# Gate, shift and scale of a conditioned trunk layer: matrix products on TensorE replaced by dot products on VectorE along a Hyena stage

## The chip, the cores and the metric

One core of a Trainium2 chip runs the whole program. The metric is the device time of one execution in microseconds (us), smaller is better. Before the change it is 3126.3 us, the median of three runs from 3124.62 to 3126.78.

The engines are named as in the profile: PE is TensorE (PEld its weight loads), DVE is VectorE, ACT is ScalarE, POOL is GpSimd, SP is SyncE, which issues most loads.

## The reference

One step of a backbone with two trunk layers, on 128 context tokens and 1024 latent tokens, model width D = 1024. Each layer first computes six vectors of width D from a condition, for the context (`c_ctx`) and for the latents (`c`):

```python
def adaln_mod(cond, w_ada, b_ada):
    m = jax.nn.silu(cond) @ w_ada + b_ada          # D -> 6 * D
    return jnp.split(m[:, None, :], 6, axis=-1)

hp = modulate(rmsnorm(xp, norm_w[i, 0]), mp[0], mp[1])
yp = mixer(hp)                                      # layer 0: hyena, layer 1: attention
xp = xp + mp[2] * rmsnorm(yp, norm_w[i, 1])
hp = modulate(rmsnorm(xp, norm_w[i, 2]), mp[3], mp[4])
xp = xp + mp[5] * rmsnorm(conv_ffn(hp, *ff), norm_w[i, 3])
```

and the same for the latents with `ms`. `modulate(h, s, c)` is `h * (1 + c) + s`. The change concerns vectors 2, 3 and 4 of layer 0: the gate of the first mixer, and the shift and the scale of the first feed-forward. The first mixer is Hyena: a product with a 1024 x 3072 matrix, a short convolution of three taps, a product of two of the three parts, a long convolution through a transform, and a product with the third part.

## The kernel before

All arithmetic is float32. A matrix product is made of three PE products, with each operand split into a rounded part `hi` and a remainder `lo`.

**The Hyena stage** is the loop `main` in `hyena()` (L1363), for j = 0 to 7 over blocks of 128 channels, with nine steps s each. In a step PE does one `group` (24 matmuls, L1340 to L1342: one third of the columns of one of the block's three parts, from the split weights `wr`). Then `short` of the group before is done: one ACT instruction (L1356) and two on DVE (L1357, L1358), from the bank in PSUM into `cb`. The rest of a step is spread over the block:

- s = 6: `Conv` multiplies two parts on DVE, `vxr` and `vxp` (through the helper at L951).
- s = 7: `turn` transposes them on PE (L1216, L1219), then `back` of the block before (L1268, L1273) goes back from the transform.
- s = 8: `base` transforms (L1232, L1237), a part of the filter network runs (L1132), and `unturn` transposes the result of the block before (L1283, L1286) into three PSUM banks.
- s = 0 of the next block: `gate` multiplies these banks with the third part on DVE (`yx`, `yxp`) and sends them off; `spread`, `mul` and `gather` are the butterflies and complex products on DVE at s = 0 to 5.

Instructions run on each engine in the order in which the code issues them. The order is written out by hand in this loop. Buffers come from pools with a planned place in memory, so an instruction may also wait for an earlier reader of the memory that it is to write.

**The vectors 2, 3 and 4** come from `Pipe` (L227) with `ada_items(0, (2, 3, 4), 2, ab1)`: 24 items, each half of the contraction of 256 of the 3072 columns. `pipe.step` starts one in steps s = 5, 6, 7 of blocks 0 to 6 and in s = 0, 1, 2 of block 7. An item loads 512 KB (`adar`, L310), two steps later splits it with two ACT instructions and an adding DMA issued by POOL (`halves`), one step later does 8 matmuls with `sc4`, the split and silu'd condition, as the stationary operand (L324), and every second item adds the bias on DVE (`m`, L331). For the gate the rows go to DRAM (L335), for shift and scale two PE transposes (L340) and two DVE instructions (L342, L343) put them into `ab`. So there are 12 additions at L331 and eight times two transposes.

Because each of these 8 matmuls goes with a `hi` or a `lo` of the condition in the four rows of `sc4`, the gate has four rows in DRAM, and `g_steps` loads and adds two halves for each of its two rows.

In a later stage the same kind of vectors is already computed in another way (`ada_rows`, L350 to L385): weights transposed, one row of 1024 per partition, and DVE multiplies a row by the broadcast condition and sums it in one instruction (L379).

Of the kernel before, what the change touches and what calls it, by code (L numbers as in the profile page):

```python
# [9 lines left out]
F32 = mybir.dt.float32  # L10
# [5 lines left out]
P = 128  # L16
# [141 lines left out]
def tile_step(tc, nc, a: dict, cst, mem, banks):  # L158
# [68 lines left out]
    class Pipe:  # L227


        def __init__(self, items):  # L230
            self.todo, self.live = iter(items), []

        def step(self, start=1):
            for g in list(self.live):
                if next(g, self) is self:
                    self.live.remove(g)
            for _ in range(start):
                g = next(self.todo, None)
                if g is not None:
                    next(g)  # L240
                    self.live.append(g)

        def drain(self, start=1):
            self.step(start)
            while self.live:
                self.step(start)


    sc4 = cst([P, KT, 4], F32R, "sc4")
    scf = cst([P, KT, 2], F32, "scf")  # L250

    def ada_setup():
        sync.dma_start(scf, a["cond"])
        act.activation(scf, scf, AF.Silu)
        split(sc4[:, :, 0:2], sc4[:, :, 2:4], scf)
# [50 lines left out]

    def ada_item(l, n, h, box, lead, ab):

        raw = bt([4, 256], "adar")
        sync.dma_start(raw, a["w_ada"][l, n, :, 4 * h:4 * h + 4, :])  # L310
        if h == 0:
            box["b4"] = st([256], "b4")[0:4]
            sync.dma_start(box["b4"], a["b_ada4"][l, :, n * 256:(n + 1) * 256])
        for _ in range(lead):
            yield
        ws = halves(raw, bt, [4, 256], True)
        del raw
        yield
        if h == 0:
            box["pt"] = ps("ada", True)  # L320
        pt = box["pt"]
        for k in range(4):
            for i, w in enumerate(ws):
                pe.matmul(pt[0:4, 0:256], sc4[:, 4 * h + k, :], w[:, k, :],  # L324
                          start=h == 0 and k == 0 and i == 0, stop=h == 1 and k == 3 and i == 1)
        del ws, w
        yield
        if h == 0:
            return
        m4 = st([256], "m4")[0:4]  # L330
        dve.tensor_tensor(out=m4, in0=pt[0:4, 0:256], in1=box.pop("b4"), op=ALU.add)  # L331
        unpin(box.pop("pt"))
        q, r = divmod(n, 4)
        if q % 3 == 2:
            pool.dma_start(m_d[l][q][:, 256 * r:256 * r + 256], m4)  # L335
            return
        yield
        pt = ps("adaT")
        for i in range(2):
            pe.transpose(pt[:, 4 * i:4 * i + 4], m4[:, P * i:P * i + P], ident[0:4, 0:4])  # L340
        m = st([2, 4], "mT")
        dve.tensor_copy(m, pt[:, 0:8].rearrange("p (i c) -> p i c", i=2))  # L342
        dve.tensor_tensor(out=ab[:, q % 3, :, 2 * r:2 * r + 2].rearrange("p c k -> p k c"),  # L343
                          in0=m[:, :, 0:2], in1=m[:, :, 2:4], op=ALU.add)

    def ada_items(l, qs, lead, ab):
        for q in qs:
            for r in range(4):
                box = {}
                for h in range(2):  # L350
                    yield ada_item(l, 4 * q + r, h, box, lead, ab)
# [55 lines left out]
    def g_steps(l, which, halves=False):  # L407

        wp = bt([D], "wp")
        sync.dma_start(wp, a["norm_w"][l, 2 * which + 1:2 * which + 2, :].partition_broadcast(P))  # L410
        gs, g2 = [bt([D], "G") for _ in range(2)], []
        src = m_d[l][3 * which + 2]
        for c in range(2):
            sync.dma_start(gs[c], src[c:c + 1, :].partition_broadcast(P))
            if halves:
                g2.append(bt([D], "g2"))
                sync.dma_start(g2[c], src[c + 2:c + 3, :].partition_broadcast(P))
        for g in gs:
            yield
            if halves:  # L420
                dve.tensor_tensor(out=g, in0=g, in1=g2.pop(0), op=ALU.add)
            dve.scalar_tensor_tensor(out=g, in0=g, scalar=32.0, in1=wp, op0=ALU.mult, op1=ALU.mult)
        yield gs
# [215 lines left out]


    SEVEN = ((0, 0), (4, 1), (5, 2), (3, 3), (1, 0), (6, 2), (2, 3))
    GROUPS = (3, 2, 2, 2, 2, 2, 2, 2, 2, 3)

    def ffn(l, hs, gs, nxt, queue, extra=iter(()), late=(), after=None):

        raw, spl, hid, accs = {}, {}, {}, {}
        ops, rows, sums, out = {}, {}, {}, {}
# [57 lines left out]
        def load_pair(j):  # L705
            if j < NJ:
                raw[j] = [bt([KT, P], "wr") for _ in range(2)]
                for i in range(2):
                    sync.dma_start(raw[j][i], a["ffn_up"][l, j, :, i])

        lo, hi = slice(0, 4), slice(4, 8)

        def total(i, j):

            a1, a2 = raw[j]
            x, y, op = ((a2[:, lo], a2[:, hi], ALU.add), (sums.get((1, j)), a1[:, lo], ALU.subtract),
                        (a1[:, lo], a2[:, lo], ALU.subtract), (a1[:, hi], sums.get((2, j)), ALU.subtract))[i - 1]
            t = sums[i, j] = bt([4, P], f"s{i}")
            dve.tensor_tensor(out=t, in0=x, in1=y, op=op)

        def weight(q, j):

            if q in (1, 2, 3, 6):
                return sums[{1: 2, 2: 3, 3: 1, 6: 4}[q], j]
            return raw[j][q == 5][:, lo if q == 0 else hi]

        def high(q, j):
            ops[j, q] = bt([4, P], "hi", F32R), bt([4, P], "lo", F32R)
            act.activation(ops[j, q][0], weight(q, j), AF.Copy)  # L729

        def low(q, j):
            dve.tensor_tensor(out=ops[j, q][1], in0=weight(q, j), in1=f(ops[j, q][0]), op=ALU.subtract)

        def both(q, j):
            ops[j, q] = halves(weight(q, j), bt, [4, P], True)

        def product(j, q):
            b, d = SEVEN[q]
            if q < 4:
                out[j, d] = ps("pp", True)  # L740
            pt = out[j, d]
            wh, wl = ops.pop((j, q))
            bh, bl = hs["pair"][b]
            for k in range(4):
                for i, (w, t) in enumerate(((wh, bh), (wh, bl), (wl, bh))):
                    pe.matmul(pt[:, 0:NP], w[:, k, :], t[:, k, :], start=q < 4 and k == 0 and i == 0,  # L746
                              stop=k == 3 and i == 2, skip_group_check=q > 3)

        def add(dst, x, pt):
            dve.tensor_tensor(out=dst, in0=pt, in1=x, op=ALU.add)  # L750

        def evac(q, j):
            if q == 0:
                u = sums["u", j] = st([NP], "u")
                act.activation(u, out[j, 0][:, 0:NP], AF.Copy)  # L755
                rows[j] = [st([2 * NP - 2], "row") for _ in range(2)]
            elif q == 1:
                pt, u = out.pop((j, 1)), sums["u", j]
# [1611 lines left out]
```

## Time and profile before

| what | us |
|---|---|
| device time, median of 3 runs | 3126.3 |
| the profiled execution | 3126.71 |
| its span, first to last instruction | 3124.9 |
| PE busy | 3044.9 (97%) |
| DVE busy | 2143.6 (69%) |
| ACT busy | 1729.7 (55%) |
| POOL busy | 619.2 (20%) |

The Hyena loop runs from about 50 to 562 us of this span, and its blocks begin (first matmul of step s = 0) at 50.79, 115.32, 176.43, 239.72, 301.21, 363.83, 431.30 and 494.07 us. These edges cut the stretches below. A row of a group of instructions gives the line, the engine, the operation, what it writes and reads, its size and, in square brackets, how long the engine sat idle before it and what ended that. A DVE instruction can start some ns before the one ahead of it has ended, so a slot is best read from start to start.

### The profile page before, as it was taken

To read this page: it belongs to the slowest core of one execution; us is meant where nothing else is said; L and a number is where in the kernel's file an instruction comes from. 1 tells how busy PE (TensorE), PEld (TensorE's weight loads), DVE (VectorE), ACT (ScalarE), POOL (GpSimd) and SP (SyncE) were. 2 spreads that over 40 slices of the span, in tenths; PEclk is the share of its full clock that TensorE was granted. 3 is DMA by queue.
4 is the path that set the end of the run, shared out by engine and by line. 5 is a ranking of instruction groups with operands and counts; after the bars stand their busy time and mean duration, and the time that the engine had idled before them with its cause. 6 is when DMAs were issued, how large, how long until landed. Compare 5 with 4: busy or idle time off the path is not lost. (4 is left out here: it accounts for less than half of the span.)

```text
span 3124.9 us, 46695 instructions
## 1 busy us (share of the span) xinstructions
PE 3044.9 (97%) x17332; PEld 2823.7 (90%) x17332; DVE 2143.6 (69%) x3057; ACT 1729.7 (55%) x3185; POOL 619.2 (20%) x1010
## 2 busy tenths in 40 slices
PE   8999999999998999999999999999999999999998
PEld 5999999778888999988899999999888998999987
DVE  5778888756676787776563347789565756777743
ACT  5454445545544777655533348899545546777532
POOL 3111111220001222211143422223220002222100
PEclk9999999999999999999999999999999999999999
DMA  6455546754445898777464464353363246887763
GB/s 254 114 125 119 125 114 157 212 187 141 149 156 154 211 214 209 168 290 258 149 196 148 134 194 110 96 145 106 135 212 140 96 161 153 215 183 182 218 212 119
DMA packets 190136, 520.48 MB, mean 167 GB/s; under 512 B 25730, under 2 KB 53986, under 8 KB 189908
## 3 DMA queue, kind: packets, MB, share of 16 engines
q1 hardware_dynamic: 137428, 394.94, 37.9%
q0 software_dynamic: 52480, 122.56, 19.5%
q8 instruction: 136, 2.23, 0.3%
q14 instruction: 92, 0.75, 0.1%
HBM read 354.50 MB, written 68.13 MB: 135 GB/s over the span
## 5 line engine op out<-in xcount | busy, mean ns | idle before, releaser
L746 PE MATMUL banks<-pair,hi 128*128 128x386 f32 x2464 | 639.1, 341 | 10.0 <-DVE junk L599 9.8
L746 PEld LDWEIGHTS banks<-pair,hi 128*128 128x128 f32 x2464 | 453.2, 190 | 11.4 <-DVE junk L599 10.7
L215 ACT ACTIVATE hi<-wr 128x1024 fp32r<-128x1024 f32 (+1 forms) x400 | 365.2, 913 | 150.4 <-DMA wr<-ffn_up 47.6
L220 DVE TENSOR_TENSOR lo<-wr,hi 128x1024 fp32r<-128x1024 f32 x247 | 305.4, 1237 | 204.8 <-ACT hi L215 203.4
L746 PE MATMUL banks<-pair,lo 128*128 128x386 f32 x1232 | 419.1, 340 | 0.7 <-DMA lo<-wr 0.7
L218 POOL DMA_DIRECT2D lo<-wr x153 | 132.5, 866 | 860.9 <-ACT lo L217 637.4
L690 PE MATMUL banks<-lo,hi 128*128 128x512 f32 x792 | 250.2, 396 | 5.9 <-DVE lo L220 5.9
L690 PE MATMUL banks<-hi,hi 128*128 128x512 f32 x792 | 251.7, 398 | 2.3 <-ACT hi L215 2.3
L690 PE MATMUL banks<-hi,lo 128*128 128x512 f32 x792 | 249.9, 395 | 0.0
L667 PE MATMUL banks<-hi,hi 128*128 128x388 f32 x704 | 240.6, 342 | 8.5 <-ACT hc L510 8.2
L669 PE MATMUL banks<-hi,lo 128*128 128x388 f32 x704 | 239.1, 340 | 1.8 <-DVE lo L220 1.8
L668 PE MATMUL banks<-lo,hi 128*128 128x388 f32 x704 | 239.7, 340 | 0.0
L746 PEld LDWEIGHTS banks<-pair,lo 128*128 128x128 f32 x1232 | 233.3, 189 | 1.0 <-DMA lo<-wr 1.0
L1746 DVE TENSOR_REDUCE mx<-banks 128x1 f32<-128x1152 f32 x128 | 173.4, 1356 | 68.9 <-PE banks L1741 61.7
L1340 PE MATMUL banks<-hi,hi 128*128 128x386 f32 (+1 forms) x576 | 200.4, 348 | 3.8 <-DVE hi L2072 2.5
L1342 PE MATMUL banks<-hi,lo 128*128 128x386 f32 (+1 forms) x576 | 197.1, 342 | 5.8 <-DMA lo<-wr 5.7
L1646 PE MATMUL banks<-hi,hi 128*128 128x384 f32 (+1 forms) x576 | 198.9, 345 | 0.0
L217 ACT ACTIVATE lo<-hi 128x512 fp32r<-128x512 f32 (+1 forms) x265 | 187.0, 706 | 18.6 <-DMA lo<-wr 6.2
L1648 PE MATMUL banks<-hi,lo 128*128 128x384 f32 (+1 forms) x576 | 196.0, 340 | 0.5 <-DVE lo L220 0.5
L1341 PE MATMUL banks<-lo,hi 128*128 128x386 f32 (+1 forms) x576 | 196.3, 341 | 0.0
L1647 PE MATMUL banks<-lo,hi 128*128 128x384 f32 (+1 forms) x576 | 195.9, 340 | 0.0
L690 PEld LDWEIGHTS banks<-lo,hi 128*128 128x128 f32 x792 | 148.8, 189 | 43.2 <-DVE lo L220 9.3
(386 smaller groups left out, 6869.5 us busy)
## 6 DMA issues: line engine op xcount, KB each, us to landing
wr<-ffn_up SPq DMA_DIRECT2D x176, 512.0 KB
wr<-ffn_down SPq DMA_DIRECT2D x132, 512.0 KB
lo<-wr POOLq DMA_DIRECT2D x132, 256.0 KB, 3.9
adaw<-w_adat SPq DMA_DIRECT2D x56, 512.0 KB
lo<-s POOLq DMA_DIRECT2D x88, 256.0 KB, 3.9
x<-x_d SPq DMA_DIRECT2D x33, 512.0 KB
hid<-cv SPq DMA_DIRECT2D x44, 384.0 KB
hd<-hid SPq DMA_DIRECT2D x88, 192.0 KB
```

The source lines that it names most:

```text
L215: act.activation(hi, src, AF.Copy)
L220: dve.tensor_tensor(out=lo, in0=src, in1=f(hi), op=ALU.subtract)
L667: pe.matmul(pt[:, 0:n], wh[:, k, :], hh[:, k, 0:n], start=k == 0, stop=False)
L668: pe.matmul(pt[:, 0:n], wh[:, k, :], hl[:, k, 0:n], start=False, stop=False)
L669: pe.matmul(pt[:, 0:n], wl[:, k, :], hh[:, k, 0:n], start=False, stop=k == KT - 1)
L690: pe.matmul(accs[c][i][h], s_[:, o:o + P], w_[:, 512 * h:512 * h + 512], start=first and n == 0, stop=last and n == len(parts) - 1)
L746: pe.matmul(pt[:, 0:NP], w[:, k, :], t[:, k, :], start=q < 4 and k == 0 and i == 0, stop=k == 3 and i == 2, skip_group_check=q > 3)
L1340: pe.matmul(pt[:, 0:n], wh[:, k, :], hh[:, k, 0:n], start=k == 0, stop=False)
L1341: pe.matmul(pt[:, 0:n], wh[:, k, :], hl[:, k, 0:n], start=False, stop=False)
L1342: pe.matmul(pt[:, 0:n], wl[:, k, :], hh[:, k, 0:n], start=False, stop=k == KT - 1)
L1646: pe.matmul(pt[:, 0:m], wh[:, k, :], hh[:, k, b:b + m], start=k == 0, stop=False)
L1648: pe.matmul(pt[:, 0:m], wl[:, k, :], hh[:, k, b:b + m], start=False, stop=k == KT - 1)
```

## The change

The three vectors are now computed by `ada_rows(0, (2, 3, 4), mcol[0])`: 24 steps, three vectors by eight blocks of 128 columns. Each loads 512 KB of the transposed weights (`adaw`, one step ahead), and DVE does two dot products, one for the context's and one for the latents' condition. The loop advances them in steps s = 0, 2, 4 and 6 of blocks 1 to 7: the first two advances load and silu the conditions (two ACT instructions), so the pairs of dot products stand in block 1 at s = 4 and 6, in blocks 2 to 6 at s = 0, 2, 4 and 6, and in block 7 at s = 0 and 2. After the loop the gate goes to DRAM by two PE transposes, one ACT instruction and one DMA (`gate_rows`), and `ab_from` builds the shift and the scale from `mcol`.

`Pipe`, its items, `sc4`, the bias `b_ada4` and the halves of the gate are gone. The code of the first product of the feed-forward is put into a class `Seven`; on DVE one sum and the preceding step's `finish` change places there, everything else stands in the same order. The core of the diff:

```diff
-    class Pipe:
-    def ada_item(l, n, h, box, lead, ab):
-        raw = bt([4, 256], "adar")
-        sync.dma_start(raw, a["w_ada"][l, n, :, 4 * h:4 * h + 4, :])
...
-        ws = halves(raw, bt, [4, 256], True)
...
-        for k in range(4):
-            for i, w in enumerate(ws):
-                pe.matmul(pt[0:4, 0:256], sc4[:, 4 * h + k, :], w[:, k, :],
...
-        dve.tensor_tensor(out=m4, in0=pt[0:4, 0:256], in1=box.pop("b4"), op=ALU.add)
...
-    def g_steps(l, which, halves=False):
+    def g_steps(l, which):
...
-        def main(filt, pipe, starts, between, tail):
+        def main(filt, rows, between, tail):
...
-                    pipe.step(starts(j, s))
+                    if j and s in (0, 2, 4, 6):
+                        next(rows, None)
...
-        pipe = Pipe(ada_items(0, (2, 3, 4), 2, ab1))
+        rows = ada_rows(0, (2, 3, 4), mcol[0])
...
-            pipe.drain(2)
-            wn = st([KT], "abw")
-            sync.dma_start(wn, a["nwc"][0, 1])
+            run(rows)
+            gate_rows(0, 2, mcol[0])
...
-            scale_ab(ab1, wn)
+            ab1 = ab_from(0, 1, mcol[0])
...
-            return op, make_g(0, 0, True), ab1
-        return main(filt, pipe, lambda j, s: 1 if s in ((0, 1, 2) if j == KT - 1 else (5, 6, 7)) else 0, between, tail)
+            return op, make_g(0, 0), ab1
+        return main(filt, rows, between, tail)
```

What a pair is, in the code that is now called here:

```python
junk = bt([D], "adaj")
for c in range(2):
    dve.scalar_tensor_tensor(out=junk if c == 0 else w, in0=w, scalar=1.0, in1=cb[c],
                             op0=ALU.mult, op1=ALU.mult, accum_out=mcol[:, q, k, c:c + 1])
```

DVE at the start of block 2, before (`m` is the bias addition, `yx` and `yxp` the gate of block 0, `hfb` the filter's taps, `fS` the first butterfly):

```order
168 L331 TENSOR_TENSOR m_1887<-banks,b_1100 4x256
169 L951 TENSOR_TENSOR yx_1907<-banks,cb_794 128x4x128 x2
170 L951 TENSOR_TENSOR yxp_1909<-banks,cb_794 128x128
171 L951 TENSOR_TENSOR hfb_1919<-banks,dec_1645 128x512 x2
172 L951 TENSOR_TENSOR fS_1936<-uA_1796,uB_1797 128x1024
```

and now, with the line numbers of the changed kernel (L1306 is `short`, L310 the dot products, L899 the helper):

```order
169 L1306 SCALAR_TENSOR_TENSOR cb_1556<-banks,hvec,cb_1556 128x384
170 L310 SCALAR_TENSOR_TENSOR adaj_1823,mcol_95<-adaw_1586,cb_1228 128x1024
171 L310 SCALAR_TENSOR_TENSOR adaw_1586,mcol_95<-adaw_1586,cb_1230 128x1024
172 L899 TENSOR_TENSOR yx_1827<-banks,cb_790 128x4x128 x2
173 L899 TENSOR_TENSOR yxp_1830<-banks,cb_790 128x128
174 L899 TENSOR_TENSOR hfb_1841<-banks,dec_1602 128x512 x2
```

The addition `m` is gone and a pair of dot products stands ahead of the gate and of everything behind it.

DVE at s = 6 of block 2, before (the last butterfly, `short`, and the product that `turn` transposes):

```order
212 L951 TENSOR_TENSOR fS_1936<-fS_1936,uA_1796 128x1024
213 L1357 SCALAR_TENSOR_TENSOR cb_2068<-banks,hvec,cb_2068 128x384
214 L1358 SCALAR_TENSOR_TENSOR cb_2068<-banks,hvec,cb_2068 128x384
215 L951 TENSOR_TENSOR vxr_2268<-cb_1857,cb_2068 128x128x8
216 L951 TENSOR_TENSOR vxp_2270<-cb_1857,cb_2068 128x128
```

and now:

```order
218 L899 TENSOR_TENSOR fS_1857<-fS_1857,uA_1728 128x1024
219 L1305 SCALAR_TENSOR_TENSOR cb_1981<-banks,hvec,cb_1981 128x384
220 L1306 SCALAR_TENSOR_TENSOR cb_1981<-banks,hvec,cb_1981 128x384
221 L310 SCALAR_TENSOR_TENSOR adaj_2189,mcol_95<-adaw_2068,cb_1228 128x1024
222 L310 SCALAR_TENSOR_TENSOR adaw_2068,mcol_95<-adaw_2068,cb_1230 128x1024
223 L899 TENSOR_TENSOR vxr_2193<-cb_1789,cb_1981 128x128x8
224 L899 TENSOR_TENSOR vxp_2195<-cb_1789,cb_1981 128x128
```

A pair stands directly ahead of `vxr`; nothing of the change stands between `vxp` and the next block's first `short`.

PE at s = 8 of block 2, before (the end of the last group, an item's matmuls, and `base`):

```order
981 L1342 MATMUL banks<-hi_764,lo_2149 128x386
982 L324 MATMUL banks<-hi_2319,sc_93 4x256
983 L324 MATMUL banks<-lo_2321,sc_93 4x256
984 L324 MATMUL banks<-hi_2319,sc_93 4x256
985 L324 MATMUL banks<-lo_2321,sc_93 4x256
986 L324 MATMUL banks<-hi_2319,sc_93 4x256
987 L324 MATMUL banks<-lo_2321,sc_93 4x256
988 L324 MATMUL banks<-hi_2319,sc_93 4x256
989 L324 MATMUL banks<-lo_2321,sc_93 4x256
990 L1232 MATMUL banks<-uT_2332,mat_457 128x128
```

and now:

```order
931 L1288 MATMUL banks<-hi_760,hi_2061 128x386
932 L1289 MATMUL banks<-lo_761,hi_2061 128x386
933 L1290 MATMUL banks<-hi_760,lo_2063 128x386
934 L1180 MATMUL banks<-uT_2243,mat_456 128x128
935 L1180 MATMUL banks<-uT_2243,mat_458 128x128
```

The item's eight matmuls are gone from PE; `base` follows the group at once.

## Rows read from the trace of the kernel before

**Rows 1.** Stretches: busy us (instructions) of PE, PEld, DVE, ACT, POOL; granted clock, DMA.

```profile
176.43:494.07 317.64, 311.83 (x2114) 303.88 (x2112) 267.02 (x469) 144.92 (x235) 48.67 (x63) 0.99 0.50 121
239.72:301.21 61.49, 61.40 (x423) 60.12 (x422) 52.72 (x92) 28.60 (x47) 10.24 (x13) 1.00 0.51 125
363.83:431.30 67.47, 64.49 (x426) 62.93 (x424) 53.37 (x94) 28.84 (x47) 10.17 (x12) 0.95 0.47 114
494.07:562.00 67.93, 65.37 (x444) 61.98 (x443) 57.23 (x103) 36.08 (x53) 12.77 (x16) 1.00 0.66 171
```

**Rows 2.** DVE's timeline in block 2: start, duration, operation [idle before].

```profile
177.28 0.40 DVE L331 TENSOR_TENSOR m<-banks,b 4x256 f32<-4x256 f32 x1
177.61 2.33 DVE L951 TENSOR_TENSOR yx<-banks,cb 128x512 f32<-128x512 f32 x2
...
181.76 1.23 DVE L951 TENSOR_TENSOR fS<-uA,uB 128x1024 f32<-128x1024 f32 x1 [0.44 <-PE banks L324]
...
185.94 0.62 DVE L1357 SCALAR_TENSOR_TENSOR cb<-banks,hvec,cb 128x385 f32<-128x385 f32 x1 [0.36 <-ACT cb L1356]
...
219.18 0.28 DVE L951 TENSOR_TENSOR vxp<-cb,cb 128x128 f32<-128x128 f32 x1
...
224.75 1.23 DVE L951 TENSOR_TENSOR fS<-kA,kA 128x1024 f32<-128x1024 f32 x1 [2.82 <-PE banks L1216]
...
239.38 0.62 DVE L1357 SCALAR_TENSOR_TENSOR cb<-banks,hvec,cb 128x384 f32<-128x384 f32 x1 [1.78 <-ACT cb L1356]
```

**Rows 3.** PE's timeline from `turn` of block 2 to block 3.

```profile
223.68 1.03 PE L1216 MATMUL banks<-ident,vxr 128*128 128x128 f32 x8
...
232.91 0.28 PE L324 MATMUL banks<-hi,sc 128*4 128x256 f32 x1
...
233.85 3.73 PE L1232 MATMUL banks<-uT,mat 128*128 128x128 f32 x32
...
239.72 0.42 PE L1340 MATMUL banks<-hi,hi 128*128 128x388 f32 x1
```

**Rows 4.** One stretch within block 2, columns as in rows 1.

```profile
188.66:219.46 30.80, 29.18 (x191) 28.55 (x190) 30.21 (x55) 8.46 (x15) 2.51 (x5) 1.00 0.52 144
```

**Rows 5.** DVE's timeline behind the loop, a pair of dot products and what follows.

```profile
620.69 1.22 DVE L379 SCALAR_TENSOR_TENSOR adaj<-adaw,cb 128x1024 f32<-128x1024 f32 x1
...
621.95 1.22 DVE L379 SCALAR_TENSOR_TENSOR adaw<-adaw,cb 128x1024 f32<-128x1024 f32 x1
...
623.10 0.32 DVE L447 CAST hi<-zero 128x8 fp32r<-128x8 f32 x3
```

**Rows 6.** Waits of PE, 100 to 640 us: total, times, longest.

```profile
PE banks L1342 <- DMA lo<-wr: 5.7, 5, 3.0
PE banks L1953 <- DMA w<-wo: 2.6, 1, 2.6
PE banks L324 <- DMA lo<-adar: 2.1, 2, 1.4
PE banks L1953 <- DMA w<-wor: 2.1, 1, 2.1
```

**Rows 7.** Two stretches in block 5, columns as in rows 1.

```profile
384.00:388.00 4.00, 2.67 (x8) 2.68 (x9) 3.93 (x6) 0.00 (x0) 0.00 (x0) 0.56 0.21 83
388.00:392.00 4.00, 4.00 (x15) 4.00 (x15) 3.90 (x6) 0.00 (x0) 0.00 (x0) 0.59 0.00 0
```

**Rows 8.** Block 7: waits of DVE up to 540.80, columns as in rows 6.

```profile
DVE cb L1357 <- ACT cb L1356: 3.7, 3, 1.8
DVE mT L342 <- PE banks L340: 1.0, 1, 1.0
DVE fS L951 <- PE banks L324: 0.8, 1, 0.8
```

**Rows 9.** DVE's timeline ahead of `turn` of block 7.

```profile
540.52 0.27 DVE L951 TENSOR_TENSOR vxp<-cb,cb 128x128 f32<-128x128 f32 x1
```

**Rows 10.** PE's timeline at `turn` of block 7.

```profile
543.96 1.04 PE L1216 MATMUL banks<-ident,vxr 128*128 128x128 f32 x8
```

More of the change, by code (lines that the diff above doesn't have):

```diff
@@ L225, in halves @@
         return hi, lo
-    class Pipe:
[L230 to L249, printed above, removed]
     scf = cst([P, KT, 2], F32, "scf")
@@ L405, in gate_rows @@
         pool.dma_start(m_d[l][q][0:2].rearrange("c (k p) -> k c p", p=P), r)
-    def g_steps(l, which, halves=False):
+    def g_steps(l, which):
         wp = bt([D], "wp")
         sync.dma_start(wp, a["norm_w"][l, 2 * which + 1:2 * which + 2, :].partition_broadcast(P))
-        gs, g2 = [bt([D], "G") for _ in range(2)], []
+        gs = [bt([D], "G") for _ in range(2)]
         src = m_d[l][3 * which + 2]
@@ L646, in ffn @@
         raw, spl, hid, accs = {}, {}, {}, {}
-        ops, rows, sums, out = {}, {}, {}, {}
+        rows = {}
         hid_d = [tc.dram_tile((P, 6 * P), F32, name=f"hid{l}_{j}") for j in range(NJ)]
@@ L702, in down0 @@
                     g == 0, g == NJ - 1)
[L705 to L747, printed above, removed]
@@ L779, in finish, with load_two, block @@
+        def load_two(j):
+            ws = [bt([KT, P], "wr") for _ in range(2)]
+            for i in range(2):
+                sync.dma_start(ws[i], a["ffn_up"][l, j, :, i])
+            return ws
+        def block(j, r, c):
+            if j not in rows:
+                rows[j] = [st([2 * NP - 2], "row") for _ in range(2)]
+            return rows[j][r][:, (NP - 1) * c:(NP - 1) * (c + 1)], slice(c, NP - 1 + c)
+        seven = Seven(NJ, NP, load_two, hs, block)
         def finish(j):
@@ L797, in side @@
                 rows[j][i] = rows.pop((j, i))
-        ALONG = (
-            ((-1, middle, 1), (0, total, 4), (-2, finish), (-1, evac, 6)),
-            ((-1, side, 1, 0), (-1, side, 1, 1), (1, both, 0), (0, high, 6), (0, evac, 0)),
-            ((3, load_pair), (-1, middle, 0), (2, total, 1), (0, low, 6), (0, evac, 1)),
-            ((1, both, 2), (-1, side, 0, 0), (2, total, 2), (0, evac, 2)),
-            ((2, high, 1), (1, both, 3), (-1, side, 0, 1), (0, evac, 3)),
-            ((2, low, 1), (1, both, 5), (0, evac, 4)),
-            ((-1, silu), (1, both, 4), (2, total, 3), (0, evac, 5)))
+        FILL = (((-1, middle, 1), (-2, finish)), ((-1, side, 1, 0), (-1, side, 1, 1)), ((-1, middle, 0),), ((-1, side, 0, 0),),
+                ((-1, side, 0, 1),), (), ((-1, silu),))
         def along(t):
             j, q = divmod(t, 7)
-            for d, fn, *args in ALONG[q]:
+            for d, fn, *args in FILL[q]:
                 if 0 <= j + d < NJ:
                     fn(*args, j + d)
+            seven.along(t)
         def along2(ts):
             for t in (next(ts), next(ts)):
-                if t >= -19:
+                if t >= Seven.FIRST:
                     along(t)
@@ L899, in main @@
                 j, q = divmod(t, 7)
-                product(j, q)
+                seven.product(j, q)
                 along(t)
@@ L1440, in main @@
             hs.clear()
[L1441 removed]
+            return tail(conv, mats)
         return hs, consts, load_mats, filter_mlp, Filter, load_w, split_w, main, yx_d
@@ L2005, in to_out @@
         return a["y_prompt"] if T == 0 else a["y_sample"][(T - 1) * P:T * P]
+    mcol = [mem([P, 6, KT, 2], F32, nm("mcol")) for l in range(2)]
     def prelude():
```

150 lines of the change are left out of this document (74 added, 76 removed).

## The prediction

> **What bounds the kernel now.** I read the stretches first, one for each block of the Hyena loop. In block 3 PE is busy for 61.40 of 61.49 us at the full clock, DVE for 52.72 and ACT for 28.60 [rows 1]: PE bounds the block, and 24 items of matmuls taken from it look like a plain gain. So the second view is the timeline of DVE within a block, to see where its other 8.8 us lie. From 188.66 to 219.46, the butterflies of block 2 up to `vxp`, DVE is busy for 30.21 of 30.80 us [rows 4]. Its idle time lies elsewhere: 2.82 us while it waits for `turn`, 1.78 ahead of the next block's first `short`, with smaller pieces between them [rows 2]. That is behind `vxp`, while PE does `turn`, `back`, the last group, `base` and `unturn`.
>
> So a block is a circle of two arcs. DVE's arc goes from the block's start, where it can take up the results of `unturn`, to the end of `vxp`: from 176.43 [rows 1] to 219.18 + 0.28 = 219.46 [rows 2], 43.0 us. Then PE's arc, from `turn` to the next block's start: 223.68 to 239.72 [rows 3], 16.0 us. In all 59.1, where the block takes 63.3. The difference, 223.68 - 219.46 = 4.2 us, is all that DVE may be late before it holds up `turn`, and all pairs of dot products stand on DVE's arc, none of them in its idle time. This decides the forecast.
>
> **The change part by part.** *Off PE.* Eight L324 matmuls take from 232.91 to 233.85, 0.94 us [rows 3]. Blocks 2 to 6 lose three items each, 2.82 us. A block without waits, block 3, then asks 61.49 - 2.82 = 58.7 us of PE; PE's arc loses one of the three and is 16.04 - 0.94 = 15.1. The waits for `lo<-adar`, 2.1 us in two [rows 6], go as well. If nothing took their place all of it would be won: 24 x 0.94 + 2.1 = 24.7 us, and a little for the 16 transposes.
>
> *Onto DVE.* A pair takes from 620.69 to 623.10, 2.41 us with its two readings of the sum [rows 5], the same form on the same 128x1024 operands. 24 of them are 57.8 us. Four in each of blocks 2 to 6: 9.64. What goes from DVE's arc: two additions `m`, 0.33 from start to start [rows 2], 0.66; and two waits, 0.44 for L324 and 0.36 for ACT [rows 2], since DVE is later there by a pair, 0.80. The arc becomes 43.0 - 0.66 - 0.80 + 9.64 = 51.2.
>
> These rows show 1.22 us for a dot product, just as long as other instructions of this size (`fS` 1.23 [rows 2]). The Trainium skill (Vector Engine (DVE) Microarchitecture Reference, section 7, Points that are easy to get wrong) says that this form with two sources in SBUF that aren't bf16 runs at half throughput. If that doubled the row's time, four pairs would take some 19 us and the block some 76; the row was taken with just such operands, so the trace already contains whatever there is of it, and I keep the row.
>
> *A block from 2 to 6.* 51.2 + 15.1 = 66.3 us, against PE's own 58.7. Before, these five took 317.64 us [rows 1]; 5 x 66.3 = 331.5, **+13.9 us**. PE now has 7.6 us in each block in which it waits. Some of that it will spend on `lo<-wr`, the remainder of the group's weights: 5.7 us in five waits before [rows 6], and PE comes 1.9 us earlier within the block, so I take 1.5 to 3.5 there. Some 0.5 to 1 goes at s = 1, where the banks of `unturn` come free a pair later because the gate is queued behind the pair. What is left, 2 to 5.5, is a wait for `vxr` at `turn`. Waits of PE ahead of DVE's arc cost nothing by themselves.
>
> *The granted clock.* They may cost something afterwards. Behind the 3.0 us wait for `lo<-wr` [rows 6] the clock stood at 0.56 and 0.59 for 8 us, with 8 and 15 matmuls [rows 7]: near the lower of its two levels, 1.2 GHz. Block 5, in which this lies, took 67.47; the other four took (317.64 - 67.47) / 4 = 62.5 [rows 1]. Of the 4.9 us between them the wait explains 2.3 to 3.0, and the slow clock about 2 to 2.6; I take 2.3. After a wait in the middle of a block this eats only slack now. After a wait at `turn` the slow matmuls lie on PE's arc, and the block grows to 68.6. With 2 to 5.5 us of wait at `turn` I count it for three of the five blocks, **+6.9 us**; bounds 0 and 5 x 2.6 = 13.
>
> *Blocks 0 and 1.* Block 0 loses one item and a wait of 2.1 - 1.4 = 0.7 [rows 6]: -1.6. In block 1 there are two pairs and no gate on DVE: 51.2 - 4.82 - 2.6 = 43.8 for its arc, the gate being `yx` and `yxp`, 2.33 + 0.28; PE needs 58.7 - 15.1 = 43.6 up to `turn`. The balance leaves about -0.5 there and -0.9 on PE's arc: together **-3.0**; bounds -4.5 and 0, since both engines arrive together.
>
> *Block 7.* `turn` came 543.96 - 494.07 = 49.9 us after the block's start [rows 1, 10], with five items of 0.94 and a 1.4 us wait [rows 6] ahead of it. DVE reached the end of `vxp` after 46.7 [rows 9]. It gains two pairs, 4.82, and loses three `m` and two pairs of L342/L343, about 1.5, and its waits inside the block, 3.7 - 1.8 (that one ends ahead of the block's start) + 1.0 + 0.8 = 3.7 [rows 8]: 46.3. PE without its items is earlier. **-3.5**; bounds -5 and -1.
>
> *What else moves.* Weight loads: 24 of 512 KB before and after, on SP's queue in other steps; 24 adding DMAs of POOL and 48 splits on ACT go, which had much room (28.60 of 61.49 [rows 1]). Behind the loop two additions of the gate's halves go, 1.2 each like other 128x1024 instructions, and two transposes and one ACT instruction come beside the out projection, which waits for weights there, 2.1 and 2.6 us [rows 6]. Those loads could come earlier, and buffers lie elsewhere in memory: **-1.0**; bounds -5 and +2. `finish` against one sum in the feed-forward: same work on DVE, beside a PE that is fed a step ahead: 0, bounds -1 and +1.
>
> **The sum.** 13.9 + 6.9 - 3.0 - 3.5 - 1.0 = +13.3 on the profiled execution's 3126.71, or 3140.0; that execution is 0.4 above the median, which changes nothing at this size.
>
> **The rivals.**
> *No slow clock at `turn`.* The same circle, but PE loses its slack in the middle of the block, in waits for `lo<-wr` and slow matmuls behind them, and comes to `turn` together with DVE. +6.4: 3133. For it: the longest such wait was already 3.0 with PE later [rows 6].
> *A slow clock at every `turn`*, and behind the one of block 1: 13.9 - 7.5 + 6 x 2.3 to 2.6 = +20 to +22, and up to +25 if waits for the new loads come on top: 3147 to 3152. For it: 7.6 us of slack must go somewhere, and one long wait of 3.0 brought the clock down [rows 6, 7]. The Trainium skill (TensorE: Matmul & The Clock Gate, section HAM oscillation — how this bites in real kernels) describes a loop which waits once in each turn and starts each burst at the throttled clock; by it this rival would be the likeliest. The trace of before has one such fall in these five blocks, so it shows the price, not that it repeats.
> *The dot products fit into DVE's idle time.* DVE's work in a block becomes 52.7 + 9.64 - 0.66 = 61.7 [rows 1], less than the 62.5 that a usual block takes. If pairs ran where DVE idles, blocks would last about 62 and PE's clock would hold: 5 x 62 - 317.64 = -7.6, with the other terms -15: 3112 to 3120, faster. It decides from the point where less than 4.2 us per block fall on DVE's arc, which would need two of the four pairs behind `vxp`. Against it: all four are issued ahead of `vxp`, the last directly ahead of `vxr`.
> *The pairs cost more than their row*, by waits for `adaw` or for an earlier reader of `adaj`'s memory: 0.5 us a pair is +10, 3150 and more.
>
> **How the numbers follow.** My forecast (some of the `turn`s with a slow clock, 3135 to 3146) 0.45; none 0.2; all 0.18; pairs that cost more, over 3152, 0.07; pairs in idle time, 3112 to 3120, 0.06; between that and the second case, by a gain behind the loop, 0.04. The likeliest gives 3140. From 3128 to 3152 the range leaves out the last three, about 0.17. A measurement tells 0.2%, 6.3 us, from no change: faster is under 3120.0, 0.06; within, up to 3132.6, takes three fifths of the case without slow clocks and the 0.04 below it, 0.16; slower 0.78.
>
> **What would show it.** Right: blocks 2 to 6 last 66 to 69 us each; DVE is busy for some 62 of them and nearly without a gap from the block's start to `vxp`; PE is busy less than 60 at full clock and waits for `vxr` at `turn`; the granted clock of these stretches falls under 1 where that wait is over 2 us; the Hyena stage is 10 to 16 us longer and the rest as it was. Wrong: `vxr` ready before PE comes to `turn`; a pair other than 2.4 us; blocks of under 63 us; or a stage behind the loop that moves by more than 5 us.

## The result and the profile after

The changed kernel takes 3145.0 us (median of four runs, 3142.1 to 3147.1) where the kernel before takes 3126.5 in the same comparison: 1.0059 times as long, 95% interval 1.0042 to 1.0077, so 18.5 us slower. The profiled execution, 3142.1 us with a span of 3139.8, is the fastest of its four; against the profiled execution of before it is 15.4 us longer.

The stretches of the Hyena loop, cut at the first matmul of each block. The first row is blocks 2 to 6 together and answers to the first of [rows 1]; then blocks 3, 4, 5. Columns as in [rows 1].

```profile
172.09:510.46 338.37, 308.38 (x1983) 303.58 (x1982) 308.02 (x533) 115.30 (x205) 28.41 (x45) 0.96 0.35 98
240.14:308.34 68.20, 60.86 (x400) 59.88 (x398) 61.71 (x108) 22.95 (x41) 5.68 (x9) 0.97 0.34 97
308.34:374.74 66.40, 60.91 (x400) 59.80 (x398) 61.58 (x107) 22.85 (x41) 5.67 (x9) 0.97 0.35 100
374.74:444.13 69.39, 63.79 (x399) 62.67 (x398) 61.69 (x108) 23.15 (x41) 5.69 (x9) 0.93 0.34 95
```

The five blocks last 338.4 us instead of 317.6. In block 3 PE was busy for 61.4 of 61.5 us before; now for 60.9 of 68.2, partly at a lower clock, and DVE for 61.7. The timeline of DVE in block 2, at its start and ahead of `vxp`, answers to [rows 2] and [rows 5]:

```profile
172.95 1.22 DVE L310 SCALAR_TENSOR_TENSOR adaj<-adaw,cb 128x1024 f32<-128x1024 f32 x1
...
174.21 1.23 DVE L310 SCALAR_TENSOR_TENSOR adaw<-adaw,cb 128x1024 f32<-128x1024 f32 x1
...
175.35 2.33 DVE L899 TENSOR_TENSOR yx<-banks,cb 128x512 f32<-128x512 f32 x2
...
218.94 1.22 DVE L310 SCALAR_TENSOR_TENSOR adaj<-adaw,cb 128x1024 f32<-128x1024 f32 x1
...
221.35 1.93 DVE L899 TENSOR_TENSOR vxr<-cb,cb 128x1024 f32<-128x1024 f32 x1
223.12 0.28 DVE L899 TENSOR_TENSOR vxp<-cb,cb 128x128 f32<-128x128 f32 x1
```

A pair takes 172.95 to 175.35 and 218.94 to 221.35, 2.40 and 2.41 us, with no wait ahead of it. From the block's start, 172.09, to the end of `vxp`, 223.40, DVE's arc is 51.3 us, where it was 43.0.

PE at `turn` of blocks 2 to 6 answers to the first of [rows 3]; before, it did not wait there:

```profile
223.34 1.06 PE L1164 MATMUL banks<-ident,vxr 128*128 128x128 f32 x6 [2.02 <-DVE vxr L899]
...
291.53 0.66 PE L1164 MATMUL banks<-ident,vxr 128*128 128x128 f32 x4 [4.37 <-DVE vxr L899]
...
359.57 0.66 PE L1164 MATMUL banks<-ident,vxr 128*128 128x128 f32 x4 [0.71 <-DVE vxr L899]
...
426.12 1.11 PE L1164 MATMUL banks<-ident,vxr 128*128 128x128 f32 x4 [3.04 <-DVE vxr L899]
...
495.29 0.87 PE L1164 MATMUL banks<-ident,vxr 128*128 128x128 f32 x6 [3.44 <-DVE vxr L899]
```

And the stretches from these five starts to the next block's start, PE's arc. The number ahead of the last two is the granted clock:

```profile
223.34:240.14 16.80, 16.80 (x122) 16.80 (x123) 11.47 (x23) 7.63 (x16) 0.39 (x1) 0.90 0.36 95
291.53:308.34 16.81, 16.81 (x123) 16.81 (x123) 11.50 (x23) 7.61 (x16) 0.39 (x1) 0.90 0.36 95
359.57:374.74 15.17, 15.17 (x123) 15.17 (x123) 11.50 (x23) 7.50 (x16) 0.34 (x1) 1.00 0.41 105
426.12:444.13 18.01, 18.01 (x122) 18.01 (x123) 11.50 (x23) 7.61 (x16) 0.38 (x1) 0.83 0.32 88
495.29:510.46 15.17, 15.17 (x122) 15.17 (x123) 11.49 (x23) 7.50 (x16) 0.39 (x1) 1.00 0.41 106
```

At full clock the arc is 15.17 us; in three of five blocks the clock fell behind the wait, and the arc is 1.6, 1.6 and 2.8 us longer. The clock in these rows is a mean over the arc: in block 5 the granted clock is 0.50, the 1.2 GHz level, from 426.12 to 432.00 and full from 434.00 on. PE's waits in these five blocks, which answer to [rows 6]:

```profile
PE banks L1290 <- DMA lo<-wr: 16.4, 7, 3.8
PE banks L1164 <- DVE vxr L899: 13.6, 5, 4.4
```

So PE has a second large wait beside the one for `vxr`: the weights' remainder `lo<-wr`, 16.4 us. Which of the two sets the block, the runs had to tell.

Behind the loop, the first matmul of the out projection comes at 572.63, before at 559.68 (L1902 and L1953 of the two kernels, from the timelines of PE):

```profile
572.63 1.20 PE L1902 MATMUL banks<-w,wo 128*128 128x512 f32 x4 [0.47 <-ACT wo L215]
```

```profile
559.68 1.20 PE L1953 MATMUL banks<-w,wo 128*128 128x512 f32 x4 [0.65 <-ACT wo L215]
```

That is +12.95 there; the span is +14.9 at its end.

### The profile page after: what moved, and what is told of

The parts are those of the page before. It is cut to its first block, busy times and chain, and to the rows that moved or that the text cites. A ratio compares the mean times of both kernels' runs of the same rounds, so it can differ in the third digit from the quotient of the medians.

```text
span 3139.8 us, 46118 instructions
## 1 busy us (share of the span) xinstructions
PE 3032.8 (97%) x17126; PEld 2815.8 (90%) x17126; DVE 2190.4 (70%) x3126; ACT 1684.2 (54%) x3139; POOL 587.0 (19%) x983
## 4 chain that ended last, share of the span: by engine, by line
PE 63%; DVE 3%; issue 2%; ACT 2%; DMA 2%; POOL 1%; SPq 0%; POOLq 0%; DVEq 0%; ACTq 0%
PE banks L629 20%; PE banks L704 15%; PE banks L1690 4%; PE banks L1721 4%; PE banks L1597 3%; PE banks L1596 3%; PE banks L1595 3%; PE banks L681 3%; PE banks L683 2%; PE banks L682 2%; PE banks L1711 2%; PE banks L1902 2%; DMA wr<-ffn_up 1%; DVE lo L220 1%; ACT hi L215 1%
## 5 line engine op out<-in xcount | busy, mean ns | idle before, releaser
L747 DVE SCALAR_TENSOR_TENSOR cv<-row,dw,cv 128x768 f32<-128x768 f32 x176 | 178.0, 1013 | 10.4 <-ACT cv L742 8.4
```

## The experiments

Each run is given with its ratio to the kernel before, measured beside it. The median of that kernel lay between 3124.6 and 3127.1 us in the five comparisons, so a difference between runs of two comparisons is uncertain by some 2.5 us.

Three theories stood against each other. **The circle:** a block is DVE's arc up to `vxp` and PE's arc behind `turn`; the pairs lengthen the first, slow clocks the second. **A:** PE's waits for `lo<-wr` set the block. **B:** the other loads or the other places of buffers in memory do.

### The pairs behind `vxp`

```diff
-                    if j and s in (0, 2, 4, 6):
-                        next(rows, None)
+                    if s in ((7, 8) if 1 < j < 7 else (0, 2, 4, 6) if j else ()):
+                        for _ in range(2 if 1 < j < 7 else 1):
+                            next(rows, None)
```

> The changed kernel with the place of the dot products alone moved: the four pairs of each of blocks 2 to 6 stand behind `vxp`, two at s = 7 and two at s = 8, where before the change DVE idled; blocks 1 and 7 as in the changed kernel. Same instructions, same loads. Theory (a block is DVE's arc up to `vxp` plus PE's arc from `turn` on, and the pairs lengthen the first): the pairs leave DVE's arc, DVE has 53.7 + 9.6 = 63.3 us of work in a block and no idle time left, blocks 2 to 6 take 62.5 to 64.5 instead of 67.7 on average, the five together about 318 instead of 338, the total 3122 to 3128, and PE no longer waits for `vxr`. Rival A (PE's waits for the weights' remainder `lo<-wr`, 18 us in all, set the block): these stay and so does the time, 3140 to 3147. Rival B (24 more loads or other places in memory): as A.

3132.3 us (3130.5 to 3133.8), 1.0022 times the kernel before (1.0013 to 1.0032): 12.7 us faster than the changed kernel, with the same instructions, but over the 3122 to 3128 expected. Blocks 2 to 6 together and block 5:

```profile
173.84:494.31 320.47, 300.76 (x1983) 297.99 (x1981) 305.69 (x527) 114.64 (x205) 28.64 (x45) 0.98 0.38 105
364.23:429.26 65.03, 60.49 (x400) 59.94 (x398) 61.66 (x108) 22.93 (x41) 5.72 (x9) 0.97 0.36 102
```

PE no longer waits for `vxr` in them. Place alone took 18 us out of the five blocks, which neither A nor B allows. But PE is busy for 60.5 of 65.0 us and DVE for 61.7, so neither fills the block: five waits for `lo<-wr`, 17.7 us, longest 4.2, and a slow clock behind them remain. So A is wrong as the cause in the changed kernel, and right as the next bound: beside these waits PE has only 2.0 us of others in the five blocks.

### No pairs at all

```diff
+            if l == 0 and qs == (2, 3, 4):
+                if n == 0:
+                    pool.memset(mcol, 0.0)
...
+                yield
+                continue
             for c in range(2):
                 dve.scalar_tensor_tensor(out=junk if c == 0 else w, in0=w, scalar=1.0, in1=cb[c],
```

The 24 pairs are passed over and their loads stay; the kernel leaves out this part of the vectors, which are zero plus the bias.

> The changed kernel without the 24 pairs of dot products; their loads stay, and the vectors are zero plus the bias, so this part of the computation is left out. Theory: DVE's arc shrinks to some 42 us, PE bounds the block again at 58.7 us and a wait of 1 to 3 for `lo<-wr`: blocks 2 to 6 take 59.5 to 62 us, together about 303 instead of 338, and block 7 some 2 less: 3104 to 3112, some 15 to 22 under the kernel before, which is what the change would bring if DVE had room. Rival A: the waits for `lo<-wr` stay at 2 to 3.8 us with slow clocks behind them, blocks 64 and more, over 3125. Rival B (the loads or places in memory): 3140 or more.

3115.6 us (3113.4 to 3119.4), 0.9973 (0.9960 to 0.9985): 8 to 9 us under the kernel before instead of the expected 15 to 22. The five blocks take 311.3 us, and in them PE waits only for one thing:

```profile
PE banks L1299 <- DMA lo<-wr: 12.3, 5, 3.2
```

The chain behind this wait can be read in the changed kernel at the start of block 3, in the timelines of DVE, ACT, POOL and PE, one line each:

```profile
248.25 1.36 DVE L899 TENSOR_TENSOR uA<-uA,uB 128x1024 f32<-128x1024 f32 x1
```

```profile
249.65 0.63 ACT L923 ACTIVATE uA<-uA 128x512 f32<-128x512 f32 x1 [9.85 <-DVE uA L899]
...
251.04 1.05 ACT L215 ACTIVATE hi<-wr 128x1024 fp32r<-128x1024 f32 x1
```

```profile
253.48 0.90 POOL L218 DMA_DIRECT2D lo<-wr  x1 [4.96 <-ACT lo L217]
```

```profile
259.64 0.44 PE L1290 MATMUL banks<-hi,lo 128*128 128x388 f32 x1 [2.97 <-DMA lo<-wr]
```

ACT scales the butterfly's half `uA` at s = 0, and waits for DVE for that; the split of the next group's weights is queued behind it, then POOL's adding DMA, and PE needs its result at s = 3. From the issue to PE's start it is 6.2 us. Before the change the same chain took 6.9 us from the issue, at 188.25, and ended 0.64 us late in block 2:

```profile
195.19 0.45 PE L1342 MATMUL banks<-hi,lo 128*128 128x388 f32 x1 [0.64 <-DMA lo<-wr]
```

Two of a block's three items of matmuls, 1.9 us, stood on PE ahead of this place; without them PE comes earlier, and these waits are 12.3 us in five blocks instead of 5.7. So the removed matmuls had been cover for a transfer, and of the 24.7 us that the prediction held possible for the matmuls and their own waits 8 to 9 were left. The next runs take this wait away.

### The split one step earlier

```diff
-                    elif c == 1:
+                    elif c == 0:
                         split_w(i + 1)
-                    elif c == 2:
+                    elif c == 1:
                         load_w(i + 2)
```

Now ACT splits ahead of the scaling. The edit was made to the changed kernel, to the one without pairs and to the kernel before.

> The changed kernel with the weights of the next group loaded and split one step earlier each, so that ACT splits ahead of the scaling that waits for DVE's butterfly at s = 0 and `lo<-wr` lands long before PE needs it. The pairs stay where the change put them. Theory (DVE's arc to `vxp`, 51.3 us, and PE's arc from `turn`, 15.1 and 16.8 to 18.0 behind a slow clock): PE no longer waits for `lo<-wr` but as much longer for `vxr`, 5 to 7 us; blocks 2 to 6 take 66.4 to 69 us as before, together 332 to 345; 3138 to 3152. Rival (in the changed kernel the waits for `lo<-wr` set the block, 14 to 18 us in all with the slow clock behind them): 3122 to 3132.

3151.4 us (3149.7 to 3151.9), 1.0081 (1.0066 to 1.0096). PE's waits in the five blocks, block 3, and PE's arc of block 2:

```profile
PE banks L1164 <- DVE vxp L899: 38.4, 5, 7.8
```

```profile
242.55:310.95 68.40, 60.55 (x400) 60.14 (x398) 61.68 (x108) 22.75 (x42) 5.73 (x9) 0.95 0.33 97
225.51:242.55 17.04, 17.04 (x122) 17.04 (x123) 11.41 (x22) 7.97 (x17) 0.00 (x0) 0.88 0.14 53
```

All of `lo<-wr` is gone, and the kernel is no faster: by the medians it is 6 us slower. This is the run that decides between the circle and A: every bit of slack now lies ahead of `turn`, 7.6 to 7.9 us in each block, the clock falls behind each of these waits, PE's arc is 16.9 to 17.0 in every block, and the five blocks take 341.4 us, each 51.3 + 17.0.

> The kernel without the pairs of dot products (their loads stay, the vectors are left without them), with the same earlier split. Theory: without the pairs the waits for `lo<-wr` had taken PE's place as the bound; without these too PE is the bound and works at full clock: blocks 2 to 6 at 58.7 to 59.5 us, together 294 to 298 where the kernel without the pairs took 311; 3097 to 3104, which is the whole 22 to 25 us of the removed matmuls. Rival (something else of the change, loads or places in memory, holds the blocks): 3110 to 3116.

3092.6 us (3090.3 to 3093.6), 0.9892 (0.9878 to 0.9907), below the expectation. Blocks 2 to 6 and block 3:

```profile
172.90:464.94 292.04, 292.04 (x1984) 291.88 (x1982) 261.23 (x453) 115.33 (x206) 30.14 (x45) 1.00 0.40 113
231.31:289.71 58.40, 58.40 (x400) 58.37 (x398) 52.32 (x92) 23.07 (x42) 6.01 (x9) 1.00 0.41 113
```

PE is busy for every moment of 292.0 us at full clock: 58.4 a block, where the prediction had worked out 58.7. The loads are those of the change, so they do not hold the loop. The buffers of the pairs live shorter here, so the places need not be the same; what speaks against these is the run before, in which the two arcs alone make up each block with all pairs in it.

> The kernel before the change with the earlier split alone. Theory: its five waits for `lo<-wr`, 5.7 us, and the one slow clock in block 5, 2 to 2.6, go; PE bounds every block of 2 to 6 at 61.4: together 307 to 309 instead of 317.6; 3115 to 3120. Rival (DVE's arc of 43 us plus PE's 16 already limits, or ACT is held up by the earlier split): 3122 to 3128.

3119.3 us (3114.4 to 3121.3), 0.9981 (0.9972 to 0.9990); the five blocks 309.6 instead of 317.6. So the earlier split gives 5 us without the change. The other 26.7 us (3119.3 to 3092.6) come from the change when its pairs are left out and nothing else holds the blocks: 24.7 had been worked out for the matmuls and their waits.

### Matmuls in PE's wait

```diff
                     pt = ps("ut")
+                    if g == 0 and 1 < self.j < 7:
+                        for i in range(24):        # the second run: range(9)
+                            pe.matmul(pt[:, 0:P], mats[0][:, i % 8, :], mats[1][:, i % 8, :], start=True, stop=True)
```

> The changed kernel with 24 more matmuls (128x128, their results unused, about 2.8 us) on PE directly ahead of `turn` in blocks 2 to 6, so that PE works while it would wait for `vxr`. Theory (behind the waits at `turn` the slow clock lengthens PE's arc in three of five blocks by 2 to 3 us): the waits fall under 2 us, no slow clock behind them, each block 66 to 66.8, the five together 331 to 334 instead of 338: 3135 to 3141, faster although PE does more. Rival (the clock behind the wait costs nothing, or another wait takes its place): 3143 to 3150, since in a block where PE came late the matmuls add up to 2.8 us.

3161.0 us (3158.9 to 3162.3). The 24 matmuls took 5.5 us instead of 2.8, since the trace shows two for each that is written, and held `turn` up themselves: it began 3.2 to 4.7 us after the end of `vxp`. The expectation fell through the size of the edit. The clock at `turn` it does show: PE has no wait there, and its arc is 15.1 us in all five blocks (228.16 to 243.27 in block 2).

> The changed kernel with 9 unused matmuls of 128x128 ahead of `turn` in blocks 2 to 6. In the run with 24 they took 5.5 us, twice as long as meant, and held `turn` up themselves; 9 take about 2.1. Theory (slow clock on PE's arc behind the wait at `turn`, 1.6 to 2.8 us in three of five blocks): waits at `turn` fall under 2 us, `turn` to the next block 15.2 in every block, five blocks together 331 to 337 instead of 338; 3137 to 3144. Rival: where PE comes late the matmuls hold `turn` up by up to 2 us, or the fall of the clock only moves to the waits for `lo<-wr`: 3144 to 3150.

3147.7 us (3145.9 to 3150.0), 1.0071 (1.0054 to 1.0087): not told apart from the changed kernel. PE's arc in four of the five blocks:

```profile
224.03:239.17 15.14, 15.13 (x121) 15.14 (x122) 11.45 (x23) 7.52 (x16) 0.35 (x1) 1.00 0.39 105
292.01:307.15 15.14, 15.14 (x125) 15.14 (x123) 10.20 (x20) 7.50 (x16) 0.00 (x0) 1.00 0.34 97
359.79:374.93 15.14, 15.14 (x124) 15.14 (x123) 10.16 (x20) 7.50 (x16) 0.00 (x0) 1.00 0.34 96
426.35:441.51 15.16, 15.16 (x123) 15.16 (x123) 11.49 (x23) 7.50 (x16) 0.35 (x1) 1.00 0.40 105
```

Where PE works up to `turn`, the granted clock stays at 1.00 behind it: the arc is 15.14 to 15.16 in every block, instead of up to 18.0. That half of the expectation held. The gain did not come: the five blocks take 336.0 instead of 338.4 and the whole no less, since the waits for `lo<-wr` grew to 21.1 us and PE, with the matmuls, came up to 1.3 us after `vxp` in some blocks. Filling the wait moved the loss to another place.

### The pairs spread

Three versions with all the work done, by the steps in which a pair is issued. The first two advances load the conditions and bring no pair, so the second version has two pairs in block 0, not the four that its expectation counts:

```
changed: block 1: 4 6;  2 to 6: 0 2 4 6;  7: 0 2
first:   block 0: 4 5 6 7 8 8;  1: 4 7 8;  2 to 6: 7 8, in blocks 2, 4, 6 two at 7;  7: 0 8
second:  block 0: 8 8;  1: 7 7 8;  2 to 6: 7 7 8;  7: 0 2 7 8;  with the earlier split
third:   block 0: 4 5 6 8;  1: 4 7 8;  2 to 6: 2 7 8;  7: 0 2;  with the earlier split
```

> The changed kernel with the 24 pairs spread to where DVE idled: six in block 0 at s = 4 to 8, three in block 1, two or three in each of blocks 2 to 6, all behind `vxp` (s = 7 and 8), two in block 7; the loads of the conditions go to block 0. Theory: DVE's work in a block is 53.7 + 2.4 x 2.41 = 59.5, about PE's own 58.7 and its waits for `lo<-wr`: blocks 2 to 6 take 59.5 to 62 us, block 0 as in the changed kernel: 3103 to 3113, faster than both kernels. Rival A (`lo<-wr`): blocks 64 and more, 3122 to 3130. Rival B: over 3135.

> All pairs, spread to where DVE idled, and the earlier split: four pairs in block 0 (s = 5, 6 and two at 8), three in each of blocks 1 to 6 behind `vxp` (two at s = 7, one at s = 8), four in block 7 (s = 0, 2, 7, 8). Theory: DVE has 53.7 + 7.2 = 60.9 us of work in a block and PE 58.7; blocks 2 to 6 take 60.5 to 62, together 303 to 310; 3102 to 3113, faster than the kernel before. Rival (waits that the pairs cause elsewhere, as `lo<-wr` did): blocks of 63 and more, 3118 to 3126.

> The earlier split and another spread of all 24 pairs: one pair each at s = 4, 5, 6, 8 of block 0, at s = 4, 7, 8 of block 1, at s = 2, 7, 8 of blocks 2 to 6, at s = 0, 2 of block 7, never two in one step, since the second of two waits for its load. Theory: DVE's arc up to `vxp` has one pair, 43.0 - 1.5 + 2.4 = 44 us, with PE's 15.1 some 59.1, next to PE's own 58.4: blocks 2 to 6 take 59 to 60.5 us, together 295 to 303; 3099 to 3108, the fastest with all the work done. Rival (the two pairs behind `vxp` hold up PE through other banks, as with three there): blocks of 61 and more, 3109 to 3116.

3122.0 us (3118.0 to 3129.5), 3115.2 (3113.4 to 3115.6) and 3114.8 (3112.1 to 3117.2); against the kernel before 0.9990 (0.9981 to 0.9999), 0.9964 (0.9951 to 0.9977) and 0.9969 (0.9958 to 0.9981). The five blocks take 308.1, 310.1 and 307.0 us. All three are faster than both kernels, the first only just, and slower than expected. In the first six pairs in block 0 held up its own `turn` by 2.5 us, and `lo<-wr` still costs 12.3 us in the five blocks; in the second PE waits 9.5 us for DVE, most of it for banks that DVE frees late, and DVE for its part idles 7.6 us ahead of the second of two pairs in one step, 4.7 of them for its load; in the third PE waits for `vxp`, 1.4 to 2.1 us in each block:

```profile
PE banks L1164 <- DVE vxp L899: 9.1, 5, 2.1
```

With one pair on its arc DVE needs 44.9 us up to the end of `vxp` (235.99 to 280.85 in block 3) instead of the 44 expected, and behind the three waits of 2.0 to 2.1 us the clock fell again: PE's arc is 16.8 us there, 15.1 behind those of 1.4 and 1.5. Against the kernel before with the earlier split, 3119.3, what the move from PE to DVE gives is 4 to 5 us by the medians, of the 26.7 that come without the pairs; the runs of both versions overlap with that kernel's, so the size is rough.

### The feed-forward

In the changed kernel the second feed-forward takes 4.5 us longer than before, which the prediction had at 0, and much the same in the others with the change. The first product of the first feed-forward, in the same code, is 1.8 us shorter (341.5 instead of 343.3 from its first start to its last). Two runs looked for the cause.

> The changed kernel with the feed-forward's one swap on DVE undone (the sum again ahead of `finish`); the Hyena stage as changed. In all kernels with the change the second feed-forward from its first group to its last down product takes 4.5 us longer than before it (first part 345.2 to 345.5 instead of 342.8, last part 183.4 instead of 181.3). Theory S (the swap does it, by its order on DVE): 342.8 and 181.3 again, 3138 to 3142. Theory M (other places of the buffers in memory or something else of the change, not the swap): 345 and 183.4 as in the changed kernel, 3142 to 3148.

```
changed, on DVE at q = 0:    middle, finish, total 4, evac 6
this run, as before:         middle, total 4, finish, evac 6
```

3146.2 us (3141.2 to 3147.7): as the changed kernel. The second feed-forward takes 344.3 us for its first part, from its first group to the last start of the first product, where the changed kernel takes 345.2 and the kernel before 342.8; and 183.4 for the last, as the changed kernel. So the swap is at most some 0.9 us of the 4.5, and not the cause of the rest.

The Hyena loop of this run is that of the changed kernel, so it shows how far executions of one loop differ. PE's arcs of blocks 3 and 5:

```profile
293.93:311.23 17.30, 17.30 (x122) 17.30 (x123) 11.49 (x23) 7.60 (x16) 0.40 (x1) 0.87 0.35 92
430.51:447.79 17.28, 17.28 (x123) 17.28 (x123) 11.49 (x23) 7.60 (x16) 0.40 (x1) 0.87 0.34 92
```

Four of its five `turn`s have a slow clock behind them, not three: the arcs are 16.78, 17.30, 16.79, 17.28 and 15.16 us. Block 2 begins at 174.55 instead of 172.09, the five blocks take 339.6 us, and the out projection comes at 576.23, 3.6 us later.

> The kernel with one pair on DVE's arc and the earlier split, instruction for instruction, with all buffers at other places in memory (the planner takes late buffers first among those of one size). The readout is the second feed-forward, which the change touches only through these places: 342.8 and 181.3 us for its two parts before the change and with the earlier split alone, where its buffers lie at the same places as before, 344.3 to 345.5 and 183.4 to 183.5 in all kernels with the change, where they lie at the same places among each other. Theory M (the places set these 4.5 us): a third pair of times, over 0.7 us away from 345.4 or 183.5 in at least one part, either way; the total between 3108 and 3122. Rival (something else of the change, as the place of the constants): 345.4 and 183.5 again, 3112 to 3117.

```diff
-    todo = np.lexsort((first, -size))
+    todo = np.lexsort((-first, -size))
```

3153.7 us (3151.1 to 3159.2), 39 us more than the same instructions at their former places. First and last start of the first product's matmuls and of the down product's, in the kernel before, the changed one and this one:

```profile
L746 PE MATMUL banks<-pair,hi x2464: 332/339/690, 990.0 to 2934.0; 128*128 128x386 f32 x190
...
L690 PE MATMUL banks<-hi,hi x792: 387/394/628, 706.7 to 3115.3; 128*128 128x512 f32 x198
```

```profile
L629 PE MATMUL banks<-pair,hi x2464: 332/339/690, 1000.7 to 2947.1; 128*128 128x386 f32 x190
...
L704 PE MATMUL banks<-hi,hi x792: 387/395/628, 717.6 to 3130.5; 128*128 128x512 f32 x198
```

```profile
L629 PE MATMUL banks<-pair,hi x2464: 332/339/691, 986.0 to 2963.7; 128*128 128x386 f32 x190
...
L704 PE MATMUL banks<-hi,hi x792: 387/392/773, 714.3 to 3143.4; 128*128 128x512 f32 x198
```

The last part, from the last start of the one to the last start of the other, takes 181.3, 183.4 and 179.7 us with the same 792 matmuls. PE waits for nothing in it in any of the three; from one start to the next it takes 229, 232 and 227 ns on average. The first part takes 342.8, 345.2 and 346.8 us. So the places alone move these stages by as much as the change did, in both directions. That the 4.5 us of the changed kernel come from its places is thereby possible and, for the last part, likely, since its buffers there lie elsewhere than before; but it is not shown for these very places.

Most of the 39 us lies elsewhere. Against the profiled execution of the same instructions at their former places the out projection comes 17.7 us later (562.05 instead of 544.31), and the first product of the first feed-forward takes 370.3 us instead of 341.5. In the five blocks of the loop DVE now waits ahead of `fTW` for PE (L1231), 10.8 us in all, where it did not; in that first product PE's waits grow from 7 to 26 us. So much of it is waits that came with the other places, and slow clocks behind them: PE's arc is 16.7 to 16.8 us in all five blocks, at the former places in three.

## Why the prediction was right

Predicted were 3140 us (3128 to 3152), measured 3145.0; slower, as forecast, by 18.5 instead of 13.3.

- **The two arcs.** DVE's arc was worked out as 51.2 us: it is 51.3 in blocks 2 to 6. PE's arc without an item, 15.1: it is 15.17. The blocks with no slow clock at `turn`, 66.40 and 66.33, are their sum, 66.3. DVE's own time in a block, 61.7, is under the 62.5 of a usual block of before, so the rival of the idle time had its numbers right; what decided against it was the place in the order, as the run with the pairs behind `vxp` shows.
- **The price of a pair**, 2.41 from the stage behind the loop [rows 5], was 2.40 and 2.41. No dot product waited for its load or its memory within these blocks, and the doubled time, which had been weighed against the row, did not come: 1.22 and 1.23 us for 1024 elements again.
- **The slow clock.** Three of five `turn`s were forecast at 2.3 us each, 6.9; it was three of five, 1.6 + 1.6 + 2.8 = 6.1. That it was three is luck: the sign that was named, a wait of over 2 us, would have given four, but 3.44 us was not followed by a fall; and with the same loop the run with the old finish has four falls, 7.5 us. How it would come about was only half right: waits for `lo<-wr`, forecast at 1.5 to 3.5 a block, are 16.4 us in five, 3.3 on average, and took so much of PE's 7.6 us of slack that one `turn` waited for 0.7 us only. Where they are gone (the earlier split) PE waits 7.6 to 7.9 us, just the slack that was worked out, and the clock falls in every block. That is the prediction's second rival, which the waits for `lo<-wr` kept away.
- **Blocks 2 to 6** together: +20.7 us, forecast 13.9 + 6.9 = 20.8. **Blocks 0 and 1**: -4.3, forecast -3.0 and its bound -4.5; in the run with the old finish it is -1.9. **Block 7**, up to the out projection: 62.2 instead of 65.6, -3.4, forecast -3.5.
- **Behind the loop** the sum was wrong in sign: -1.0 forecast, +2.0 in the profiled executions. The out projection and its neighbours are 2.3 us shorter, within the bounds; the second feed-forward is 4.5 longer, where the prediction put "0, bounds -1 and +1"; what lies between them cancels. The step that failed here is the term for the feed-forward: it priced the edit by its instructions on DVE alone. The order on DVE makes at most 0.9 us of it; the places of the buffers, which the prediction took into the bounds of another term, can make the rest, but what makes it stays open.
- **The rest of the difference**, 3.1 us between 15.4 in the profiled executions and 18.5 between the medians, lies in executions that were not profiled, since the profiled one was the fastest of its four. The run with the old finish shows that the same loop can take 3.6 us longer up to the out projection, 2.5 of them ahead of block 2; whether that is what happened in those executions stays open.
- **What the prediction did not see** is that its own upper limit of the gain, 24.7 us "if nothing took their place", was not to be had by making DVE free: without any pairs the kernel came only 8 to 9 us under the one before, because the matmuls had covered the transfer of `lo<-wr`. It named the wait, and costed it in the slack only.

## What to carry to other kernels

Before work is moved from the busy engine to an idle one, find where in the cycle the idle time lies: what counts is the arc between two hand-overs, and here an instruction put ahead of a hand-over cost its full time however idle the engine was behind it. Work on the busy engine may be the cover of a transfer, so with every removed instruction ask which wait it was long enough to hide, and mend that chain too (here by a split one step earlier) before judging the move. A change of buffers shifts places in memory for all stages, and here the places alone moved untouched stages by 2 to 4 us, so a few us in such a stage are no evidence on the change itself.

## What was not expected of the hardware

- A wait of 3.44 us at `turn` of block 6 left the clock at 1.00, while one of 2.02 us in block 2 was followed by 0.90 over PE's arc. So the length of a single wait did not decide alone whether the clock fell; the waits of 7.6 to 7.9 us were followed by a fall each time.
- A stage of 792 matmuls, in which PE waits for nothing, took 183.4 us in the kernel with one pair on DVE's arc and 179.7 with the same instructions and its buffers at other places in memory; in the kernel before it took 181.3. By what the places act on the matmuls no run shows. Much of the 39 us that the whole program took longer at these places is waits of one engine for another.
